# An encoder layer in split float32: one group of adaLN dots, one DMA queue and one weight-splitting step are moved

## The chip, the cores and the metric

The kernel runs on one core of one Trainium2 chip. The metric is the device time of one execution in microseconds (us); lower is better. Five engines with their own instruction streams share the work: TensorE (PE, matrix products), VectorE (DVE), ScalarE (ACT), GpSimd (POOL) and SyncE (SP, which here only starts DMA transfers). Each engine runs its stream in order, and a DMA that an engine starts waits in that stream until the buffer it writes is free.

## The reference

One layer over 1024 positions of width 1024. All arrays are float32.

```python
mod = silu(c) @ w_ada + b_ada                     # adaLN: 6 vectors of 1024
sh1, sc1, gt1, sh2, sc2, gt2 = split(mod, 6)
h = rmsnorm(x, norm1_g) * (1 + sc1) + sh1
u, v, q, k, va, gate_a, gate_b = split(h @ w_in)
a_out = gmlp_branch(u, v, ...) @ w_a              # mixing in chunks of 128 positions
b_out = window_attention_branch(q, k, va, ...) @ w_b
merged = sigmoid(gate_a) * a_out + sigmoid(gate_b) * b_out
x = x + gt1 * (merged @ w_o)
h2 = rmsnorm(x, norm2_g) * (1 + sc2) + sh2
f_gate, f_up = split(h2 @ w_ffn_in)               # 2 x 2816 columns
x = x + gt2 * ((silu(f_gate) * f_up) @ w_ffn_out)
```

## The kernel before

**Products.** Every float32 operand of a product is split into a high part, rounded to the matrix engine's float32r, and a low part, the rest. A product is then three matmuls: high by high, high by low, low by high (`mm3`). The split of a weight tile of 128 x 1024 is a "unit": SP loads it into a tile `raw`, ACT casts it into `wh`, DVE (now and then POOL) subtracts into `wl`. The three tags have three buffers each, so a unit's cast waits until the products of the unit three before it are done, and its load until that one's subtraction is done. The gates and the feed-forward use a Strassen scheme: seven block products for eight, with sums of blocks made on DVE before and after.

**Stages, in the order of time (us from the span's start).** Both halves of the sequence (512 positions each) go through projections, attention and gMLP in `half(0)` and `half(1)` (to about 394). Each ends with the *branch projections*: a loop over eight output tiles `d`, with two products of twelve matmuls a tile and one unit of `w_ab` a tile. Next come the *gates* for `d` = 2 to 7 (to about 522), by `gate_step(d, i)` for seven block products and `gate_evict(d, i)` behind each. In a gate tile DVE also splits the next tile's weights (`gate_prep_a/b/c`, `gate_sums`) and takes dot products for adaLN: `ada_half` multiplies two half rows of `w_ada` (tiles `hs`, 128 x 512) by silu(c) and sums them into one column of `mod`. A column's next rows are loaded when its `hs` buffers are free, that is, after the dots before. In tiles 3 to 5 a third `ada_half` stands between the two parts, `low_b` and `low_s`, that `gate_prep_b` leaves for the end of the tile.

Then the *output projections* (about 515 to 617): eight tiles for half 0, eight for half 1, with 24 matmuls each and one unit of `w_o` a tile. A tile's end on DVE is `x1 = gate * product + x`; the rows of x come into a tile `xs` with two buffers (L1360, `load`, SP's queue). ACT squares x1 and DVE adds the squares into `ss`; four matmuls by `ones` (`col_rstd`) turn the `ss` of half 0 into the norm, ahead of half 1's second tile. POOL's queue carries the merged rows (`hs<-md`), the stores of x1 (`x1d`) and, in three pieces of 1 MB, more rows of `w_ada`.

The *feed-forward's first product* (about 617 to 1052, over 22 tiles `f`) ends hidden tiles (`hid`) that POOL's queue stores (`tA`, `tB`), while DVE also forms sums of the output weights (`wo`, stored to `wS`). From f = 6 on, `gain_dots` works off the last eight columns of adaLN, those of gt2: rows loaded by SP into two `t` tiles, multiplied by silu(c) on POOL (`G.tensor_tensor`), summed by an ACT copy with an accumulator, finished by two small DVE instructions. The *second product* (about 1052 to the end) has 77 steps `n` of twelve matmuls; `split_step(n + 4)` splits what step n + 4 needs, `fetch(n + 12)` loads for step n + 12.

**What sets the order.** In both feed-forward products the order is written out by hand (`manual_schedule`). Elsewhere a scheduler orders each engine's stream, except where `in_order[0]` is set: there an engine keeps the order of the program. `load` (SP) always keeps that order; `store` (POOL) leaves it to the scheduler.

Of the kernel before, what the change touches and what calls it, by code (L numbers as in the profile page):

```python
# [8 lines left out]
F32 = mybir.dt.float32  # L9
# [3 lines left out]
ALU = mybir.AluOpType  # L13
# [25 lines left out]
def kernel(  # L39
# [96 lines left out]
    def load(dst, src):  # L136
        tc.keep_in_program_order(nc.sync.dma_start(dst, src))
# [13 lines left out]
    def raw_unit(src):  # L151
        r = wpool.tile([P, UNIT], F32, tag="raw", name=nm("raw"))
        load(r, src)
        return r
# [401 lines left out]
    def x_rows(hf, k):  # L556
        return xT[k * P : (k + 1) * P, hf * HALF : (hf + 1) * HALF]
# [4 lines left out]
    def added(dst, src):  # L562
        V.tensor_tensor(dst, dst, src, op=ALU.add)
# [103 lines left out]
    def gate_prep_b(d):  # L667
        w, low = begin_split(raws[d][1])
        h, l, s1 = tmp(F32R), tmp(F32R), raws[d][2]
        A.copy(h, s1)  # L670
        gunits[d] += [w, None, (h, l)]

        def rest():
            r = raws[d][0]
            added(r[:, :Q], s1)
            added(r[:, Q:], r[:, :Q])
            V.tensor_tensor(l, s1, h.bitcast(F32), op=ALU.subtract)

        return low, rest

# [51 lines left out]
    def half(hf):  # L732
# [425 lines left out]

        for d in range(KT):
            in_order[0] = d < 2 or hf == 1 and d > 5  # L1160
            if 0 < d < KT - 1:
                wab.append(unit(None, V, abr.pop(0)))
                if d + 2 + hf < KT:
                    abr.append(raw_unit(w_ab[d + 2 + hf]))
            elif d:
                if hf == 0:
                    early.append(unit(None, V, early_raw[0]))
                else:
                    for low in gate_prep_b(2):
                        low()  # L1170
            if hf and d == 5:
                gate_load(2)
            if hf and d == 6:
                gate_prep_a(2)
                gate_sums(2)
            ms = []
            for br, t in ((1, (oH, oL)), (0, (gH, gL))):
                if hf and d == KT - 1 and br == 0:
                    held.append((wab[d], t))
                    continue  # L1180
                pb = mm_bank()
                for k in range(4):
                    kc = slice(br * Q + k * P, br * Q + (k + 1) * P)
                    mm3(pb, (wab[d][0][:, kc], wab[d][1][:, kc]), (t[0][:, k, :], t[1][:, k, :]),
                        k == 0, k == 3)
                if d < 2:
                    sg = gates.pop(0)
                    V.scalar_tensor_tensor(out=sg, in0=sg, scalar=1.0, in1=pb, op0=ALU.add,
                                           op1=ALU.mult)
                    ms.append(sg)  # L1190
                else:
                    c = tmp()
                    A.copy(c, pb)
                    j = 2 * hf + br
                    nc.scalar.dma_start(pd[d][:, j * Q : (j + 1) * Q], c)
            if d < 2:
                V.tensor_tensor(ms[0], ms[0], ms[1], op=ALU.add)
                store(md[hf][d], ms[0])
            in_order[0] = hf == 1 and (d < 1 or d > 5)
            while jobs and jobs[0][0] <= d:  # L1200
                jobs.pop(0)[1]()
            in_order[0] = False
            if hf == 0:
                ada_next(d < 1)
                if d > 5:
                    early_raw.append(raw_unit((w_q[0], w_kv[0])[d - 6]))
# [33 lines left out]
    for d in range(2, KT):  # L1240
        last = d == KT - 1
        in_order[0] = True
        if d == 2:
            gate_step(d, 0)
            gate_evict(d, 0)
            held_projection()
            block_sums(3, 1, kinds)
            gate_step(d, 1)
            low_c = gate_prep_c(d)
            gate_evict(d, 1)  # L1250
            low_c()
            gate_load(d + 1)
            gate_step(d, 2)
            gate_evict(d, 2)
            branch_load(d)
            branch_load(d + 1)
            gate_step(d, 3)
            gate_evict(d, 3)
            gate_prep_a(d + 1)
            gate_step(d, 4)  # L1260
            gate_evict(d, 4)
            gate_sums(d + 1)
            low_b, low_s = gate_prep_b(d + 1)
            gate_step(d, 5)
            gate_evict(d, 5)
            low_b()
            low_s()
            continue
        gate_step(d, 0)
        gate_evict(d, 0)  # L1270
        gate_step(d - 1, 6)
        low_c = gate_prep_c(d)
        gate_evict(d - 1, 6)
        low_c()
        ada_half("hs" if not last else None)
        if not last:
            gate_load(d + 1)
        gate_step(d, 1)
        gate_evict(d, 1)
        gate_step(d, 2)  # L1280
        gate_evict(d, 2)
        if d > 2:
            if last:
                m0.extend(m_tiles(midt))
                for k in range(2):
                    m_load(m0, 0, k)
                m_src[6] = tmp()
                gating(d - 1, None, m_src[6])
            else:
                gating(d - 1)  # L1290
        if not last:
            branch_load(d + 1)
            ada_half("hs")
        gate_step(d, 3)
        gate_evict(d, 3)
        if not last:
            gate_prep_a(d + 1)
        else:
            wo_next = unit(w_o[0], V)
            for k in (0, 1):  # L1300
                m_split(m0, k)
                m_load(m0, 0, k + 2)
        gate_step(d, 4)
        gate_evict(d, 4)
        if not last:
            gate_sums(d + 1)
            low_b, low_s = gate_prep_b(d + 1)
        else:
            m_split(m0, 6)
            for k in (2, 3):  # L1310
                m_split(m0, k)
                m_load(m0, 0, k + 2)
            m_src[7] = tmp()
            gating(d, 0, m_src[7])
        gate_step(d, 5)
        gate_evict(d, 5)
        if not last:
            low_b()
            if d in (3, 4, 5):
                ada_half("hs")  # L1320
            low_s()
    in_order[0] = False
    for k in (4, 5, 7):
        m_split(m0, k)
# [5 lines left out]
    for hf in range(2):  # L1330
# [14 lines left out]
        for d in range(KT):  # L1345
# [11 lines left out]
            if hf == 1 and d in (2, 4):  # L1357
                early.append(first_unit(d // 2 - 1))
            xk = stream("xs")
            load(xk, x_rows(hf, d))  # L1360
            pw = mm_bank()
            for k in range(KT):
                if hf == 1 and (d, k) == (1, 0):
# [340 lines left out]
                            for x in "hl"]  # L1704
            split2(raws[n], *ready[n])

    again, dots = [], []

    def gain_dots(f, i):
        if f == EARLY and i == 0:  # L1710
            again.extend(stream("hs") for _ in range(2))
            for j in range(2):
                dma(again[j], silu_d[:, j * 512 : (j + 1) * 512])
        if f >= EARLY and ada_queue and i == 6:
            again[2:] = [tmp(), tmp()]
            for j in range(2):
                dma(again[2 + j], w_ada2[ada_queue[0][0] - GT1][:, j * 512 : (j + 1) * 512])
        if dots and i % 2:
            dots.pop(0)()
        if f > EARLY and ada_queue and i in (2, 4):  # L1720
            j = i // 2 - 1
            col = ada_queue[0][0]
            part = sm(16, "part")[:, :1]
            row = again[2 + j]
            G.tensor_tensor(row, row, again[j], op=ALU.mult)
            dots.append(lambda: A.activation(row, row, AF.Copy,
                                             accum_out=part if j else acc_mod[:, col : col + 1]))
            if j:
                dots.append(lambda: (added(acc_mod[:, col : col + 1], part), ada_end(col)))
                ada_queue.pop(0)  # L1730

    with tc.manual_schedule():
        U[4, 0], U[5, 0], U[0, 0], U[1, 0] = early
# [45 lines left out]
        for f, i in steps:  # L1779
# [13 lines left out]
                evict(f, i)  # L1793
            if (f, i) == (0, 5):
                evict(0, 6)
            gain_dots(f, i)
            if i == 6 or (f, i) == (0, 5):
                hidden_sums(f)
            elif f > 2:
# [1 line left out]
            if f >= EARLY:  # L1801
                e, p = divmod(7 * (f - EARLY) + i, 10)
                if e < NP and p == 0:
                    load_out(e)
                if e < NP and p == 5:
                    later.extend(lambda e=e, p=p: out_sums(e, p) for p in range(4))
            if f == NF - 1 and i > 4:
                split_step(i - 5)

# [59 lines left out]
                put(1, hf, d)  # L1869

        ngt = sm(4, "ngt")
        V.tensor_scalar(ngt, mod[:, GT2 + 4 : GT2 + 8], -1.0, None, op0=ALU.mult)

        def step_mm(n, d):
            i, e = work[n]
# [8 lines left out]
        for n, (i, e) in enumerate(work):  # L1884
# [10 lines left out]
                        step_mm(m, d)  # L1895
            split_step(n + 4)
            fetch(n + 12)
            if n in (8, 24, 40, 52):
                m = (8, 24, 40, 52).index(n)
                load_acc(m // 2, m % 2)  # L1900
# [74 lines left out]
```

## Time and profile before

| | |
|---|---|
| median of 3 runs | 1264.94 us (1264.44 to 1266.01) |
| profiled execution | 1269.63 us, span 1267.9 us |
| PE busy | 1228.1 us, 97% of the span |
| DVE busy | 919.5 us, 73% |
| ACT busy | 586.0 us, 46% |
| POOL busy | 198.9 us, 16% |
| mean granted PE clock | 0.994 |
| DMA | 236.28 MB, 186 GB/s over the span |

In a row of the timeline the first number is the start, the second the length, and the bracket at the end the idle time of that engine just before it with what ended it. In nearly all rows the line of the source is 76, that of a helper through which instructions are issued, so rows are told apart by their tiles: `wl<-raw,wh` is the low part of a unit, `mm` and `at` are PSUM banks. A matmul row of 0.39 us overlaps the next one: what counts for the rate is the distance of their starts.

### The profile page before, as it was taken

The page shows a single profiled execution, that of the slowest core. Times are in us where ns is not written, and L with a number is a line of the kernel's source. Part 1 is how long each engine was busy: PE and PEld are TensorE (multiplying, and loading weights), DVE is VectorE, ACT ScalarE, POOL GpSimd, SP SyncE. Part 2 cuts the span into 40 slices and gives each one's busy share as a digit, 9 for nine tenths or more (in the row PEclk, how much of TensorE's full clock was granted, in tenths as well). Part 3 has the DMA queues.
Part 4 walks back from the last instruction along what each step waited for, and adds up shares of the span by engine and source line. Part 5 has one row for each costly group of instructions (what it writes and reads, how often), then busy time and mean ns, then how long its engine had stood idle before and what let it go on. Part 6 is the DMA issues. An engine that isn't in the chain of part 4 may idle for free.

```text
span 1267.9 us, 15678 instructions
## 1 busy us (share of the span) xinstructions
PE 1228.1 (97%) x5634; PEld 1013.0 (80%) x5634; DVE 919.5 (73%) x1516; ACT 586.0 (46%) x970; POOL 198.9 (16%) x234
## 2 busy tenths in 40 slices
PE   5999999999999999999999998999999999999998
PEld 4888888888877877777788887778888888888887
DVE  8998884588887889775797756777766676455646
ACT  5468863367866323433454333433432334433341
POOL 1233430113441010211100011121210000010001
PEclk9999999999999999998999999999999999999999
DMA  9632168321266466765612454556644549885542
GB/s 365 261 100 77 57 213 300 120 82 51 75 197 226 133 232 213 275 215 201 258 34 100 170 195 166 183 204 222 238 164 172 195 166 337 290 322 196 188 162 100
DMA packets 78687, 236.28 MB, mean 186 GB/s; under 512 B 9361, under 2 KB 9361, under 8 KB 72594
## 3 DMA queue, kind: packets, MB, share of 16 engines
q1 hardware_dynamic: 57602, 146.67, 33.4%
q0 software_dynamic: 17552, 82.32, 18.0%
q10 hardware_dynamic: 3456, 6.29, 1.3%
q8 instruction: 44, 0.72, 0.2%
q14 instruction: 33, 0.27, 0.1%
HBM read 177.58 MB, written 57.67 MB: 186 GB/s over the span
## 4 chain that ended last, share of the span: by engine, by line
PE 72%; DVE 12%; DMA 8%; issue 4%; ACT 4%; SPq 0%; POOL 0%; ACTq 0%; DVEq 0%; POOLq 0%
PE at L76 37%; PE mm L76 35%; DVE mid L76 3%; DVE wl L76 3%; DMA raw<-in_w_o_dram 2%; ACT wh L76 2%; DMA raw<-in_w_ga_dram 1%; DMA mid<-in_w_ada_dram 1%; DVE ws L76 1%; DMA hs<-md 1%; DMA hs<-x1d 1%; DVE hid L76 1%; DMA wS<-wo 1%; DVE xs L76 1%; ACT lb L76 1%
## 5 line engine op out<-in xcount | busy, mean ns | idle before, releaser
L76 ACT CAST wh<-raw 128x1024 fp32r<-128x1024 f32 x155 | 162.2, 1050 | 175.5 <-PE mm L76 46.4
L76 DVE TENSOR_TENSOR wl<-raw,wh 128x1024 fp32r<-128x1024 f32 x141 | 172.0, 1222 | 90.5 <-ACT wh L76 87.3
L76 PE MATMUL mm<-mid,wh 128*128 128x512 f32 x696 | 215.6, 391 | 4.5 <-ACT xs L76 3.6
L76 PEld LDWEIGHTS mm<-mid,wh 128*128 128x128 f32 x696 | 130.2, 188 | 33.9 <-ACT xs L76 4.9
L76 PE MATMUL at<-j,wh 128*128 128x512 f32 x464 | 143.1, 390 | 0.1
L76 PE MATMUL mm<-mid,wl 128*128 128x512 f32 x348 | 135.7, 391 | 0.8 <-POOL wl L76 0.5
L76 PE MATMUL mm<-wh,h 128*128 128x512 f32 x384 | 129.2, 398 | 3.0 <-ACT h L76 3.0
L76 PEld LDWEIGHTS at<-j,wh 128*128 128x128 f32 x464 | 87.0, 188 | 18.6 <-ACT wh L76 0.5
L76 DVE TENSOR_TENSOR wl<-ws,wh 128x1024 fp32r<-128x1024 f32 (+1 forms) x55 | 66.0, 1200 | 44.3 <-ACT wh L76 44.3
L76 PE MATMUL mm<-j,wh 128*128 128x512 f32 x288 | 91.1, 398 | 0.3 <-ACT wh L76 0.3
L76 PE MATMUL at<-j,wl 128*128 128x512 f32 x232 | 90.4, 390 | 0.5 <-DVE wl L76 0.5
L76 PE MATMUL at<-h,wh 128*128 128x512 f32 x288 | 90.4, 396 | 0.0
L76 PEld LDWEIGHTS mm<-wh,h 128*128 128x128 f32 x384 | 71.5, 189 | 17.7 <-ACT h L76 3.9
L76 PE MATMUL mm<-h,wh 128*128 128x512 f32 x272 | 84.6, 392 | 0.0
L76 ACT CAST wh<-ws 128x1024 fp32r<-128x1024 f32 (+1 forms) x55 | 53.5, 973 | 63.0 <-DVE ws L76 49.9
L76 PEld LDWEIGHTS mm<-mid,wl 128*128 128x128 f32 x348 | 65.3, 188 | 16.0 <-DVE wl L76 1.6
L76 PE MATMUL mm<-wl,h 128*128 128x512 f32 x192 | 75.9, 395 | 0.0
L76 PEld LDWEIGHTS mm<-j,wh 128*128 128x128 f32 x288 | 55.2, 193 | 12.2 <-ACT wh L76 0.7
L76 PEld LDWEIGHTS at<-h,wh 128*128 128x128 f32 x288 | 54.5, 190 | 11.9 <-DVE mid L76 0.7
L76 DVE TENSOR_TENSOR ol<-raw,oh 128x1024 fp32r<-128x1024 f32 x30 | 36.7, 1224 | 32.7 <-ACT oh L76 32.7
L76 PEld LDWEIGHTS mm<-h,wh 128*128 128x128 f32 x272 | 50.6, 188 | 10.3
L76 PE MATMUL mm<-j,wl 128*128 128x512 f32 x144 | 57.3, 398 | 1.1 <-DVE wl L76 1.1
(279 smaller groups left out, 2564.2 us busy)
## 6 DMA issues: line engine op xcount, KB each, us to landing
raw<-in_w_gate_dram SPq DMA_DIRECT2D x28, 512.0 KB, 3.9
tA<-hid POOLq DMA_DIRECT2D x11, 1024.0 KB, 5.2
tB<-hid POOLq DMA_DIRECT2D x11, 1024.0 KB, 5.6
wo<-in_w_out_dram POOLq DMA_DIRECT2D x22, 512.0 KB, 6.2
wS<-wo POOLq DMA_DIRECT2D x11, 1024.0 KB, 5.2
raw<-wS SPq DMA_DIRECT2D x44, 256.0 KB, 3.0
raw<-tB SPq DMA_DIRECT2D x44, 256.0 KB, 3.3
raw<-in_w_out_dram SPq DMA_DIRECT2D x33, 256.0 KB, 5.1
```

The source lines that it names most:

```text
L76: ins = f(*args, **kw)
```

## The change

Four edits. (1) In `half(1)` the unit for branch tile d + 2, not d + 1, is split in tile d, and its load is started one tile earlier; `half(0)` stays. (2) In `gate_prep_b` the subtraction into `l` goes ahead of the two sums, and in tiles 3 to 5 `low_s` goes ahead of the third `ada_half`. (3) The rows of x for the output projections are loaded through POOL's queue instead of SP's. (4) The dots of gt2 leave the first product. In the second, `row_load` fetches a column's two half rows at fixed steps, and two DVE instructions that multiply and accumulate, one in each of two steps, replace the POOL multiply and the ACT sum.

```diff
@@ gate_prep_b
         def rest():
             r = raws[d][0]
+            V.tensor_tensor(l, s1, h.bitcast(F32), op=ALU.subtract)
             added(r[:, :Q], s1)
             added(r[:, Q:], r[:, :Q])
-            V.tensor_tensor(l, s1, h.bitcast(F32), op=ALU.subtract)
@@ half: branch projections
-            if 0 < d < KT - 1:
+            if 1 - hf <= d < KT - 1 - hf:
                 wab.append(unit(None, V, abr.pop(0)))
-                if d + 2 + hf < KT:
-                    abr.append(raw_unit(w_ab[d + 2 + hf]))
-            elif d:
+                if d + 2 + 2 * hf < KT:
+                    abr.append(raw_unit(w_ab[d + 2 + 2 * hf]))
+            if d == KT - 1:
@@ gates, end of a tile
             low_b()
+            low_s()
             if d in (3, 4, 5):
                 ada_half("hs")
-            low_s()
@@ output projections
-            load(xk, x_rows(hf, d))
+            store(xk, x_rows(hf, d))
@@ feed-forward, first product
-    def gain_dots(f, i):
...
-            G.tensor_tensor(row, row, again[j], op=ALU.mult)
-            dots.append(lambda: A.activation(row, row, AF.Copy,
-                                             accum_out=part if j else acc_mod[:, col : col + 1]))
...
+    AT = ((-1, 2), (7, 12), (9, 15), (14, 18), (24, 30), (30, 36), (36, 42), (42, 48))
+    def row_load(g):
+        rows2[g] = [stream("xs") if g % 2 else tmp() for _ in range(2)]
+        for j in range(2):
+            dma(rows2[g][j], w_ada2[GT2 + g - GT1][:, j * 512 : (j + 1) * 512])
...
+            if (f, i) == (NF - 2, 6):
+                row_load(0)
@@ feed-forward, second product, after fetch(n + 12)
+        def gain_dots(n):
+            for g, (at, to) in enumerate(AT):
+                if n == at:
+                    row_load(g)
+                if n in (to, to + 1):
+                    j, col = n - to, GT2 + g
+                    part = sm(16, "part")[:, :1]
+                    row = rows2[g][j]
+                    V.scalar_tensor_tensor(out=row, in0=row, scalar=1.0, in1=again[j],
+                                           op0=ALU.mult, op1=ALU.mult,
+                                           accum_out=part if j else acc_mod[:, col : col + 1])
+                    if j:
+                        added(acc_mod[:, col : col + 1], part)
+                        ada_end(col)
```

SP's queue at the start of the output projections, before: `raw` is a weight tile of `w_o`, `xs` holds rows of x.

```order
L137 DMA raw_4999<-in_w_o_dram 128x1024
L137 DMA raw_5078<-in_w_o_dram 128x1024
L137 DMA xs_5084<-in_xT_dram 128x512
L137 DMA raw_5123<-in_w_o_dram 128x1024
L137 DMA xs_5129<-in_xT_dram 128x512
L137 DMA raw_5168<-in_w_o_dram 128x1024
```

The same place of the same queue now:

```order
L137 DMA raw_4999<-in_w_o_dram 128x1024
L137 DMA raw_5078<-in_w_o_dram 128x1024
L137 DMA raw_5123<-in_w_o_dram 128x1024
L137 DMA raw_5168<-in_w_o_dram 128x1024
L137 DMA raw_5215<-in_w_o_dram 128x1024
L137 DMA raw_5260<-in_w_o_dram 128x1024
```

Between two weight tiles no load of x stands any more.

DVE where half 0's output projections end, before: `t_1066` is x1 of half 0's last tile, `ss_5077` its sum of squares, `raw_5489` and `raw_5535` are units of `w_o` for half 1, `raw_5541` is a tile of the feed-forward's gate weight, and `ms_5503<-at_5498` reads what `col_rstd` left.

```order
L76 SCALAR_TENSOR_TENSOR t_1066_5430<-mm_5405,mod,xs_5403 128x512
L76 TENSOR_TENSOR wl_5492<-raw_5489,wh_5491 128x1024
L76 TENSOR_TENSOR ss_5077<-ss_5077,t_1067_5432 128x512
L76 SCALAR_TENSOR_TENSOR mid_5446<-mm_5461,mod,xs_5459 128x512
L76 TENSOR_SCALAR ms_5503<-at_5498 128x4
L76 TENSOR_TENSOR wl_5538<-raw_5535,wh_5537 128x1024
L76 TENSOR_TENSOR j_5451<-raw_5541,j_5450 128x1024
```

And now:

```order
L76 SCALAR_TENSOR_TENSOR t_1066_5430<-mm_5405,mod,xs_5403 128x512
L76 TENSOR_TENSOR wl_5492<-raw_5489,wh_5491 128x1024
L76 TENSOR_TENSOR j_5451<-raw_5541,j_5450 128x1024
L76 TENSOR_TENSOR ss_5077<-ss_5077,t_1067_5432 128x512
L76 SCALAR_TENSOR_TENSOR mid_5446<-mm_5461,mod,xs_5459 128x512
L76 TENSOR_SCALAR ms_5503<-at_5498 128x4
L76 TENSOR_TENSOR wl_5538<-raw_5535,wh_5537 128x1024
```

The split of the gate weight now stands ahead of the last sum of squares; on ACT its cast likewise stands ahead of the last square.

POOL in the feed-forward's first product, before: `t<-t,hs` is the multiply of `gain_dots`, the rest starts transfers.

```order
L1412 DMA wS<-wo_6715 128x2048
L1412 DMA wo_6910<-in_w_out_dram 128x1024 x2
L76 TENSOR_TENSOR t_1275_6826<-t_1275_6826,hs_6711 128x512
L1412 DMA tA<-hid_6822 128x2048
L76 TENSOR_TENSOR t_1295_6968<-t_1295_6968,hs_6710 128x512
L1412 DMA tB<-hid_6829 128x2048
L76 TENSOR_TENSOR t_1296_6969<-t_1296_6969,hs_6711 128x512
```

And now:

```order
L1412 DMA wS<-wo_6711 128x2048
L1412 DMA wo_6899<-in_w_out_dram 128x1024 x2
L1412 DMA tA<-hid_6818 128x2048
L1412 DMA tB<-hid_6821 128x2048
L1412 DMA wo_7087<-in_w_out_dram 128x1024 x2
```

POOL computes nothing in this stage any more; its transfers keep their order.

More of the change, by code (lines that the diff above doesn't have):

```diff
@@ L1705, in split_step @@
             split2(raws[n], *ready[n])
-    again, dots = [], []
-    def gain_dots(f, i):
[L1710 to L1724, printed above, removed]
-            G.tensor_tensor(row, row, again[j], op=ALU.mult)
-            dots.append(lambda: A.activation(row, row, AF.Copy,
-                                             accum_out=part if j else acc_mod[:, col : col + 1]))
-            if j:
-                dots.append(lambda: (added(acc_mod[:, col : col + 1], part), ada_end(col)))
-                ada_queue.pop(0)
+    AT = ((-1, 2), (7, 12), (9, 15), (14, 18), (24, 30), (30, 36), (36, 42), (42, 48))
+    again, rows2 = [], {}
+    def row_load(g):
+        rows2[g] = [stream("xs") if g % 2 else tmp() for _ in range(2)]
+        for j in range(2):
+            dma(rows2[g][j], w_ada2[GT2 + g - GT1][:, j * 512 : (j + 1) * 512])
     with tc.manual_schedule():
@@ L1795 @@
                 evict(0, 6)
-            gain_dots(f, i)
             if i == 6 or (f, i) == (0, 5):
@@ L1806 @@
                     later.extend(lambda e=e, p=p: out_sums(e, p) for p in range(4))
+            if (f, i) == (NF - 3, 0):
+                again.extend(stream("hs") for _ in range(2))
+                for j in range(2):
+                    dma(again[j], silu_d[:, j * 512 : (j + 1) * 512])
+            if (f, i) == (NF - 2, 6):
+                row_load(0)
             if f == NF - 1 and i > 4:
@@ L1871 @@
         ngt = sm(4, "ngt")
-        V.tensor_scalar(ngt, mod[:, GT2 + 4 : GT2 + 8], -1.0, None, op0=ALU.mult)
+        def gain_dots(n):
[12 more added lines that the diff above has]
+                        ada_end(col)
+            if n == 54:
+                V.tensor_scalar(ngt, mod[:, GT2 + 4 : GT2 + 8], -1.0, None, op0=ALU.mult)
         def step_mm(n, d):
@@ L1897 @@
             fetch(n + 12)
+            gain_dots(n)
             if n in (8, 24, 40, 52):
```

## The prediction

> **What bounds the kernel now.** I read the page's busy line first, then the table by stage, then what PE waited for, then the chain and the timeline at each wait.
>
> ```profile
> PE 1228.1 (97%) x5634; PEld 1013.0 (80%) x5634; DVE 919.5 (73%) x1516; ACT 586.0 (46%) x970; POOL 198.9 (16%) x234
> ```
> ```profile
> core 0: us, PE busy (x) PEld busy (x) DVE busy (x) ACT busy (x) POOL busy (x), PEclk, DMA share, GB/s
> 345.00:410.00 65.00, 62.95 (x292) 51.20 (x291) 52.93 (x77) 43.66 (x68) 19.83 (x20) 1.00 0.64 215
> 410.00:516.00 106.00, 101.93 (x445) 82.96 (x444) 91.32 (x159) 36.77 (x51) 9.90 (x18) 1.00 0.55 184
> 516.00:576.00 60.00, 54.90 (x234) 43.46 (x234) 42.51 (x64) 23.89 (x34) 13.13 (x23) 0.98 0.80 267
> 576.00:630.00 54.00, 52.94 (x229) 43.36 (x229) 33.48 (x44) 22.16 (x29) 6.07 (x9) 0.93 0.60 219
> 730.00:860.00 130.00, 123.52 (x540) 100.65 (x539) 92.08 (x121) 46.39 (x77) 22.91 (x28) 1.00 0.53 191
> 860.00:1052.00 192.00, 192.00 (x847) 158.48 (x845) 131.78 (x185) 69.50 (x105) 24.58 (x37) 1.00 0.53 188
> 1052.00:1268.00 216.00, 210.29 (x924) 173.09 (x923) 121.70 (x123) 83.61 (x84) 10.60 (x18) 1.00 0.64 229
> ```
>
> PE sets the time, and no matmul is removed. From 860 to 1052 it never pauses: 847 matmuls in 192.00 us, 0.227 us each. Elsewhere it can only win back pauses. They are span less busy: 2.05 us in the branch projections, 4.07 in the gates, 5.10 and 1.06 in the output projections, 6.48 in the early feed-forward. Together that is 18.8 us, and the summary of PE's waits from 345 to 1052 names what ended them; its largest rows:
>
> ```profile
> PE at L76 <- DVE ss L76: 5.3, 2, 4.2
> PE at L76 <- DVE mid L76: 4.1, 3, 1.5
> ...
> PE mm L76 <- ACT xs L76: 3.6, 3, 1.7
> ```
>
> The columns are total, times, longest. All four edits aim at these rows. Besides, the clock column falls to 0.93 behind the longest wait.
>
> **Output projections (x's rows on POOL's queue).** The chain through the longest wait:
>
> ```profile
> 564.39 0.67 DVE t L76
> ...
> 565.08 0.33 SPq L137
> ...
> 565.50 4.78 DMA raw<-in_w_o_dram
> ...
> 572.58 0.69 DVE ss L76
> ```
> ```profile
> 562.59 0.73 PE L76 MATMUL mm<-j,wh 128*128 128x512 f32 x2 [0.27 <-ACT wh L76]
> 563.85 0.50 PE L76 MATMUL mm<-j,wl 128*128 128x512 f32 x1 [0.53 <-DVE wl L76]
> 573.32 1.59 PE L76 MATMUL at<-ones,ss 128*128 128x1 f32 x8 [4.20 <-DVE ss L76]
> ```
>
> SP starts the load of x's rows only when DVE has used up the older `xs`. The next `w_o` load stands behind it on SP. ACT's cast waits 4.78 us for that load, and the last square stands behind the cast. The loop closes on itself: the late unit holds back the next x1 on DVE. With x on POOL, SP is held only by its three `raw` buffers, and the `w_o` weights come well ahead. So 0.27, 0.53 and most of 4.20 us go.
>
> What is late next: the new order puts the split of a feed-forward gate weight ahead of the last square. Call T the end of half 0's last product; a tile is 24 x 0.227 = 5.44 us. That weight's load waits for the `raw` of a unit that is cast when the tile before ends (T - 5.44) and subtracted some 2.3 us later.
>
> ```profile
> L76 ACT CAST wh<-raw 128x1024 fp32r<-128x1024 f32 x155 | 162.2, 1050 | 175.5 <-PE mm L76 46.4
> L76 DVE TENSOR_TENSOR wl<-raw,wh 128x1024 fp32r<-128x1024 f32 x141 | 172.0, 1222 | 90.5 <-ACT wh L76 87.3
> ```
> ```profile
> raw<-in_w_gate_dram SPq DMA_DIRECT2D x1, 512.0 KB, 5.7
> ```
>
> With 5.7 us to land it is there at T + 2.7; cast (1.05), subtraction (1.22) and sum (0.69) give T + 5.7, and PE asks at T + 5.44. I leave 0.8 us of wait (0 to 2). The gain is 5.0 - 0.8 = 4.2 us.
>
> The clock comes on top:
>
> ```profile
> 574.77 1.20 PE L76 MATMUL mm<-j,wh 128*128 128x512 f32 x2
> ...
> 580.03 0.85 PE L76 MATMUL mm<-j,wh 128*128 128x512 f32 x2
> ```
> ```profile
> 623.25 1.02 PE L76 MATMUL at<-ones,ss 128*128 128x1 f32 x8 [1.06 <-DVE ss L76]
> 624.13 0.71 PE L76 MATMUL at<-h,wh 128*128 128x512 f32 x2
> ...
> 628.61 1.05 PE L76 MATMUL at<-ident,rcol 128*128 128x128 f32 x8
> ```
>
> Behind the pause of 4.20 us twelve matmuls take 580.03 - 574.77 = 5.26 us, not 2.72: 2.5 us lost. Behind the pause of 1.06 us twelve take 4.48: 1.8 us lost. So a short pause beside the one-column matmuls may cost too. I count 1.9 of the 2.5 us as won (bounds 0.7 and 2.5), since the new pause is nearer to none than to 1.06. The Trainium skill ("TensorE: Matmul & The Clock Gate", "Why this matters for your kernels") drops the clock only for idle gaps of more than about 3 us; by that rule all 2.5 us would be won, and the sum would be 0.6 us better. The row at 623.25 speaks against it: 1.06 us was enough there. This stage: 4.2 + 1.9 = 6.1 us (3.0 to 7.5).
>
> **Feed-forward, first product (dots leave POOL and ACT).**
>
> ```profile
> 806.55 3.96 DVE L76 TENSOR_TENSOR wl<-ws,wh 128x1024 fp32r<-128x1024 f32 x1 [0.51 <-ACT wh L76]
> ```
> ```profile
> 806.89 2.54 POOL L76 TENSOR_TENSOR t<-t,hs 128x512 f32<-128x512 f32 x2
> ```
> ```profile
> 842.12 0.63 ACT L76 ACTIVATE t<-t 128x512 f32<-128x512 f32 x1 [3.62 <-POOL t L76]
> ```
> ```profile
> 777.94 0.69 DVE L76 TENSOR_TENSOR hid<-hid 128x512 f32<-128x512 f32 x1 [5.47 <-DMA wS<-wo]
> ```
> A subtraction of 1.22 us takes 3.96 while POOL multiplies (2.54 us); PE's pause behind it is one of the 3.6 us on `xs`. At 842 ACT waits 3.62 us for POOL's product with a weight cast queued behind. Both go. The largest pause, 2.3 us, has another root: DVE waits 5.47 us for the store of `wS`, which moves beside the dots' rows; of that I leave 1.0 us. Gain: 6.48 - 1.0 = 5.4 us (3.0 to 6.5). From 860 on, with dots still running, there are no pauses, so nothing is won there.
>
> **Branch projections (units two tiles ahead).**
>
> ```profile
> 363.20 1.20 PE L76 MATMUL mm<-mid,wh 128*128 128x512 f32 x4 [0.61 <-ACT wh L76]
> 364.66 0.50 PE L76 MATMUL mm<-mid,wl 128*128 128x512 f32 x1 [0.27 <-DVE wl L76]
> 406.21 0.50 PE L76 MATMUL at<-j,wl 128*128 128x512 f32 x1 [0.53 <-DVE wl L76]
> ```
> ```profile
> 357.18 0.69 DVE L76 SCALAR_TENSOR_TENSOR t<-t,mm 128x512 f32<-128x512 f32 x1 [1.21 <-PE mm L76]
> ```
>
> The first late unit is now split a tile earlier, where DVE idles 1.21 us anyway; its 1.22 us is hidden there. If that cover fails, tile 0's evictions come 1.2 us later, still ahead of tile 2. This wins 0.88 us. Of the 0.53 at 406 I count 0.3: the earlier `l` frees the `t` tile that ACT's copy ahead of that unit's cast waits for. Gain 1.2 us (0.3 to 1.4).
>
> **Gates (`low_s` first).**
>
> ```profile
> 437.35 0.69 DVE L76 SCALAR_TENSOR_TENSOR hs<-hs,silu_c 128x512 f32<-128x512 f32 x1 [1.47 <-DMA hs<-in_w_ada_dram]
> ```
> ```profile
> 451.01 3.01 PE L76 MATMUL at<-j,t 128*128 128x512 f32 x12 [1.44 <-DVE mid L76]
> ...
> 471.52 3.02 PE L76 MATMUL at<-j,t 128*128 128x512 f32 x12 [1.17 <-DVE mid L76]
> ...
> 492.80 3.01 PE L76 MATMUL at<-j,t 128*128 128x512 f32 x12 [1.45 <-DVE mid L76]
> ```
>
> PE waits three times for an eviction on DVE, behind a backlog. Swapping two pieces of the same backlog wins only where DVE idled: in tile 3, whose dots waited 1.47 us for their rows while `low_s` could have run. That takes away the 1.44; 1.17 and 1.45 stay. The dots now start 1.9 us later, so the next dots' rows come later too; against that I set 0.2 us. Gain 1.2 us (0 to 4.1).
>
> **Second product (dots on DVE).** Sixteen multiplies of 0.69 us (the row at 437.35 is the same operation), their accumulator reads and small ends make about 1.9 us a column, 15 us in all; DVE is busy 121.70 of 216 us there, and splits run four steps (10.9 us, a step of twelve matmuls being 2.72) ahead. I put 0.3 us on the path (0 to 3); without that cover it would be up to 15. The rows' loads are 0.5 MB a column, eight times, among 229 GB/s.
>
> **Sum.** 6.1 + 5.4 + 1.2 + 1.2 - 0.3 = 13.6 us. The profiled execution is 1269.63 us (span 1267.9), so 1256.0 by it; the runs' median is 1264.94, which gives **1251.3 us**.
>
> **Rivals.** (a) Later waits take the place: the gate weight lands late, the clock still falls, `wS` holds DVE as before. With the low ends of the two large terms (3.0 and 3.0) the gain is 8.1 or less, about half of mine on balance: 1258. For it speaks that DVE stays busy 86% of the gate stage; against it, that PE's pauses end after 860. Chance 0.20.
>
> (b) Slower: POOL's queue brings x late. `xs` has two buffers, so rows are started after the x1 two tiles before and have 10.9 - 0.75 - 1.1 = 9 us until needed. If they land later, x1 waits on DVE, with the next unit's subtraction queued behind it, and PE stops in every tile. Rows of that size on POOL's queue took 4.0 us:
>
> ```profile
> hs<-md POOLq DMA_DIRECT2D x14, 256.0 KB, 4.0
> ```
>
> For a loss of over 0.2% the sixteen tiles must lose 13.6 + 2.5 = 16.1 us, 1 us each: landing in 10 us. Then it gives 1268. Chance 0.07.
>
> (c) The dots don't hide in the second product: 8 x 1.9 = 15 us on the path eats the gain, 1266. Against it speak DVE's idle 94 us. Chance 0.04.
>
> **Numbers.** My forecast has 0.69. Its own bounds and most of (a) make the range, 1246.5 to 1260. Faster by over 0.2% (2.5 us, about what a measurement of this kernel can tell): 0.69 + (a) less a little, 0.87. Within: (c) and the tail of (a), 0.05. Slower: (b) and some of (c), 0.08.
>
> **What would show it.** Right: the row `at<-ones,ss` near 570 waits under 1 us; from 730 to 860 PE is busy over 128 of 130 us; two of the three `at<-j,t` waits remain. Wrong: `xs<-in_xT` on POOL landing in over 9 us, DVE waiting for it, or PE pausing before 1100.

## The result, and the profile after

The changed kernel takes 1253.25 us (median of 5 runs, 1249.84 to 1257.47) against 1264.94 us for the kernel before. The ratio is 0.9908, with a 95% interval of 0.9883 to 0.9933: 11.6 us less, where 13.6 were forecast. Its profiled execution took 1254.18 us (span 1252.4 us), near its median; the one of before had been 4.7 us over its own, so the two profiles differ by 15.5 us, more than the kernels do.

The busy line of the changed kernel's page and its table by stage (the last stretch begins 16 us earlier now, as that stage does):

```profile
PE 1222.5 (98%) x5634; PEld 1011.4 (81%) x5634; DVE 915.0 (73%) x1548; ACT 578.7 (46%) x938; POOL 184.6 (15%) x234
```
```profile
345.00:410.00 65.00, 63.23 (x294) 51.40 (x293) 52.52 (x77) 43.89 (x69) 19.97 (x20) 1.00 0.67 212
410.00:516.00 106.00, 104.30 (x457) 85.11 (x456) 93.54 (x162) 38.38 (x53) 12.05 (x22) 1.00 0.61 204
516.00:576.00 60.00, 56.70 (x239) 46.35 (x238) 41.34 (x62) 24.30 (x33) 17.99 (x31) 0.94 0.81 273
730.00:860.00 130.00, 129.44 (x570) 106.53 (x570) 84.97 (x119) 44.91 (x62) 11.73 (x22) 1.00 0.54 194
1036.00:1252.00 216.00, 210.74 (x927) 173.26 (x925) 134.52 (x171) 84.12 (x85) 10.62 (x18) 1.00 0.68 247
```

The early feed-forward has become whole: 0.56 us without work where 6.48 were. The gates went from 4.07 to 1.70. The output projections still miss 3.30. Their clock column reads 0.94 where 0.98 stood, but only because the slow matmuls, behind 576 us before, now fall inside the stretch: over 516 to 630 us it is 0.96 before and 0.97 now. The second product is busy 210.74 us with 927 matmuls, as before (210.29 with 924). The summary of what PE waited for from 345 to 1037 names the rest:

```profile
PE at L76 <- DVE ss L76: 3.3, 1, 3.3
PE mm L76 <- ACT mid L76: 0.8, 1, 0.8
PE at L76 <- DVE mid L76: 0.6, 1, 0.6
```

One wait stands out, and it is the one that was to go. The chain through it:

```profile
556.31 0.06 DVE t L76
...
556.98 1.23 DVE wl L76
...
558.22 6.74 DMA raw<-in_w_gate_dram
...
564.98 1.05 ACT j L76
...
566.06 0.56 DVE j L76
566.62 0.58 issue
567.20 0.69 DVE ss L76
...
567.94 1.50 PE at L76 x8
```

The loop through x's rows is gone from it. The load of the feed-forward gate weight has taken its place: it starts when the subtraction at 556.98 has freed its `raw`, and takes 6.74 us; its cast and subtraction stand ahead of the last sum.

### The profile page after: what moved, and what is told of

The parts are those of the page before. It is cut to its first block, busy times and chain, and to the rows that moved or that the text cites. A ratio compares the mean times of both kernels' runs of the same rounds, so it can differ in the third digit from the quotient of the medians.

```text
span 1252.4 us, 15649 instructions
## 1 busy us (share of the span) xinstructions
PE 1222.5 (98%) x5634; PEld 1011.4 (81%) x5634; DVE 915.0 (73%) x1548; ACT 578.7 (46%) x938; POOL 184.6 (15%) x234
## 4 chain that ended last, share of the span: by engine, by line
PE 63%; DVE 11%; DMA 11%; issue 9%; ACT 5%; POOL 1%; SPq 0%; ACTq 0%; DVEq 0%; POOLq 0%
PE at L76 34%; PE mm L76 29%; DVE mid L76 3%; DVE wl L76 3%; ACT wh L76 2%; DMA raw<-in_w_out_dram 1%; DMA raw<-in_w_ga_dram 1%; DMA hs<-in_w_ada_dram 1%; DVE hs L76 1%; DMA mid<-in_w_ada_dram 1%; DMA xs<-in_w_ada_dram 1%; DVE t L76 1%; ACT lb L76 1%; DVE raw L76 1%; DMA hs<-in_xT_dram 1%
## 5 line engine op out<-in xcount | busy, mean ns | idle before, releaser
L76 DVE TENSOR_TENSOR wl<-ws,wh 128x1024 fp32r<-128x1024 f32 (+1 forms) x55 | 62.0, 1127 | 44.0 <-ACT wh L76 44.0
L76 ACT ACTIVATE xs<-xs 128x512 f32<-128x512 f32 x21 | 13.3, 633 | 96.9 <-DVE xs L76 96.9
```

Of the source, the lines that this page charges most:

```text
L76: ins = f(*args, **kw)
```

## The experiments

Stage by stage, worked out from PE's rows: the us between the same two matmuls of its stream, less those in the first profile of before (negative: shorter). The stages begin at the matmuls that stood there at 345, 410, 516, 640 and 1052 us; each column is one profiled execution. The last matmul of the gates here is the one ahead of the stop near 513 us, so that stop counts with the output projections:

```
                   before  changed  low_   x_on_  dots_  dots_first  branch_two  gate_   branch_  both_   x_two
                   again            first  pool   moved  _on_dve     _ahead      later   undone   mended  _on_sp
branch projections   0.03   -0.29  -0.47   0.04  -0.01    -0.01       -0.04       0.05   -0.42   -0.41   -0.46
gates                1.70   -4.25  -4.24  -1.35  -1.70    -3.91       -2.58      -3.30   -4.06   -4.43   -3.46
output projections  -4.36   -4.56  -3.28  -6.95  -3.30    -4.99       -2.65     -11.11   -3.39  -10.20  -12.31
first product       -0.71   -7.13  -0.13   0.02  -7.18    -1.41       -0.48      -7.00   -6.99   -6.96   -7.81
second product       0.04    0.00  -0.03  -0.02   0.08    -0.03        0.02       0.08    0.12    0.12    0.08
```

The first column is the kernel before against itself: the gates and the output projections move by 2 and 4 us from one execution to the next, the feed-forward by under 1. A profile alone therefore decides only in the feed-forward; elsewhere the runs' ratios have to.

**The kernel before again (before_again).** 

> The kernel before, unchanged, profiled once more. It tells which of the pauses in its first profile belong to the kernel and which to that one execution (1269.63 us, 4.7 us over the median). Theory (the first profile was an unlucky one): the slow matmuls behind half 1's ones-matmuls (1.8 us) are absent, as they are in three kernels that left the output projections' queues alone, and the three waits of the gate stage are smaller by 1 to 2 us in all; the five pauses of the feed-forward's first product and the pause of about 4.2 us in the output projections stay. Rival (all of it is the kernel's): every pause comes back within 0.3 us.

A second set of runs gave a ratio of 1.0013 (1.0001 to 1.0025) to the first, so 0.13% is nothing here. PE's rows in the output projections and in the gates:

```profile
574.78 1.87 PE L76 MATMUL at<-ones,ss 128*128 128x1 f32 x8 [4.18 <-DVE ss L76]
576.51 1.20 PE L76 MATMUL mm<-j,wh 128*128 128x512 f32 x2
...
580.87 0.63 PE L76 MATMUL mm<-j,wh 128*128 128x512 f32 x2
...
623.23 1.02 PE L76 MATMUL at<-ones,ss 128*128 128x1 f32 x8 [0.44 <-DVE ss L76]
```
```profile
452.42 3.01 PE L76 MATMUL at<-j,t 128*128 128x512 f32 x12 [1.63 <-DVE mid L76]
472.92 3.01 PE L76 MATMUL at<-j,t 128*128 128x512 f32 x12 [1.17 <-DVE mid L76]
494.11 4.61 PE L76 MATMUL at<-j,t 128*128 128x512 f32 x12 [1.85 <-DVE mid L76]
```

The wait of 4.2 us belongs to the kernel. The one of half 1 is 0.44 instead of 1.06 us, and no slow matmuls follow it: the 1.8 us lost there in the first profile were that execution's. On the gates the expectation was wrong: all three waits are there, 4.65 us together against 4.06, and the twelve matmuls behind the last take 4.61 us where the others take 3.01: the clock fell there (last section).

**The four edits one by one**, each alone in the kernel before.

x's rows on POOL's queue (x_on_pool):

```diff
-            load(xk, x_rows(hf, d))
+            store(xk, x_rows(hf, d))
```

> The kernel before with only x's rows on GpSimd's queue. Theory (each edit acts in its own stage): PE's two short waits before half 0's last product go (0.27 and 0.53 us), the long one before the ones-matmuls shrinks only from 4.2 to about 3.3 us, because the split of the feed-forward gate weight now stands ahead of the last square; the 1.06 us wait of half 1 and the slow matmuls behind it (1.8 us) go, because the weights of w_o come ahead there too. Gain 4.5 us in the output projections, nothing elsewhere. Rival (the output projections gained because the gate stage ended earlier): the 1.06 us wait stays, gain under 2 us.

Ratio 0.9965 (0.9951 to 0.9979), 4.4 us. From 520 to 640 us PE waits 2.60 us ahead of the ones-matmuls and nowhere else:

```profile
570.25 1.05 PE L76 MATMUL at<-ones,ss 128*128 128x1 f32 x8 [2.60 <-DVE ss L76]
571.17 0.71 PE L76 MATMUL mm<-j,wh 128*128 128x512 f32 x2
...
575.52 0.70 PE L76 MATMUL mm<-j,wh 128*128 128x512 f32 x2
```

The gain is as the theory had it, but its profile shows why no single row proves the size: half 1's wait is absent here, and in the kernel before it was 1.06 us in one profile and 0.44 in the other.

The dots alone (dots_moved), with the AT steps, `row_load` and `gain_dots` as in the diff of the change:

> The kernel before with only the gt2 dots moved to the second product. Theory: all five pauses of PE in the first product (6.5 us by the busy table, 7.3 by the matmuls' starts) go down to under 1.3 us together, the one behind the store of wS too, since the small transfers and POOL's multiplies were what made them; nothing is added in the second product. Gain 6 to 7 us. Rival (the wS pause is fixed by the time at which the stage starts, which the other edits shift): it stays at 2.3 us, gain 4 us. Rival (sixteen multiplies on DVE cost in the second product): PE pauses of 0.69 us appear between steps 2 and 49.

Ratio 0.9955 (0.9942 to 0.9969), 5.7 us. The five pauses of the first product come to 0.2 us in all, the one behind `wS` being gone too, and the second product does not change (0.08 us). The first theory holds, 0.3 us under its lower end.

`low_s` and the subtraction first (low_first), the two hunks on the gates:

> The kernel before with only the subtraction and low_s ahead of the sums and the dots. Theory (the swap wins wherever the evictions waited for the dots' backlog): all three waits before at<-j,t (1.44, 1.17, 1.45 us) fall to 0.6 us in all, gain 3.5 us, and about 1 us is given back at the end of the stage by a new wait on ACT. Rival (the recorded forecast): only the first of the three goes, gain 1.2 us.

Ratio 0.9974 (0.9963 to 0.9986), 3.3 us. One wait is left of three:

```profile
472.60 3.02 PE L76 MATMUL at<-j,t 128*128 128x512 f32 x12 [0.57 <-DVE mid L76]
```

In this profile nearly all is gone, against the forecast's one of three. The profile alone doesn't carry that: dots_first_on_dve (below) leaves the gates as they were, and its gates are 3.91 us shorter too, with waits of 0.56 and 0.34 us. Over all twelve profiles PE's waits ahead of `at<-j,t` add up to 0.90 to 4.65 us in the six without the swap (mean 2.98) and to 0 to 1.53 us in the six with it (mean 0.72). The ratio's interval, 1.8 to 4.7 us, leaves out the forecast 1.2. The wait on ACT at the end of the stage did not come with this edit.

The branch units two tiles ahead (branch_two_ahead), the first hunk of `half`:

> The kernel before with only half 1's branch units split two tiles ahead. Theory (one late unit is exchanged for another): the waits of 0.61 and 0.27 us in tile 2 go, and waits of 0.2 and 0.53 us appear at the last unit of the stage, where DVE works off the gates' first sums; net within 0.4 us of nothing. Rival (the recorded forecast): gain 1.2 us, no new wait.

Ratio 1.0017 (1.0002 to 1.0031), no more than the kernel before shows against itself. The 0.61 and 0.27 us in tile 2 are gone, and the changed kernel's PE rows show what came:

```profile
398.86 0.73 PE L76 MATMUL mm<-j,wh 128*128 128x512 f32 x2 [0.17 <-ACT wh L76]
400.12 0.50 PE L76 MATMUL mm<-j,wl 128*128 128x512 f32 x1 [0.53 <-DVE wl L76]
...
406.65 0.50 PE L76 MATMUL at<-j,wl 128*128 128x512 f32 x1 [0.53 <-DVE wl L76]
```

0.88 us saved, 0.70 added, and the 0.53 at 406 not touched. The four ratios add up to 0.9911, the whole change measured 0.9908: no sign that the edits get in each other's way.

**Mending what was left.** The gate weight's two pieces one tile later in the changed kernel (gate_later):

```diff
-            if hf == 1 and d in (2, 4):
+            if hf == 1 and d in (3, 5):
                 early.append(first_unit(d // 2 - 1))
```

> The changed kernel with the two pieces of the feed-forward gate weight split one tile later, which puts the first behind the last square and sum of half 0. Theory (PE waits 3.3 us only because the load of that weight ends late and stands ahead of the last sum): the sum is ready before half 0's last product ends, the wait falls under 0.3 us, and the slow matmuls behind it (2.5 us) go with it; gain 5.5 us. Rival (the one-column matmuls slow the clock with or without a wait): the 2.5 us stay, gain 3.3 us. Rival (the last x1 itself is late): a wait over 2 us stays, gain about 1 us.

1249.19 us, 0.9878 (0.9864 to 0.9891) of the kernel before: 4.1 us under the changed kernel. PE's rows:

```profile
566.34 0.95 PE L76 MATMUL at<-ones,ss 128*128 128x1 f32 x8
567.15 0.70 PE L76 MATMUL mm<-j,wh 128*128 128x512 f32 x2
...
570.00 0.62 PE L76 MATMUL mm<-j,wh 128*128 128x512 f32 x2
```

No wait; the next twelve matmuls take 570.00 - 567.15 = 2.85 us. In the changed kernel twelve took 574.56 - 569.29 = 5.27:

```profile
567.94 1.50 PE L76 MATMUL at<-ones,ss 128*128 128x1 f32 x8 [3.30 <-DVE ss L76]
569.29 1.20 PE L76 MATMUL mm<-j,wh 128*128 128x512 f32 x2
...
574.56 0.92 PE L76 MATMUL mm<-j,wh 128*128 128x512 f32 x2
```

So the load in front of the sum was the cause, and the slow matmuls go with the wait; the one-column matmuls by themselves cost nothing. The stage gains 6.6 us between the two profiles, by the runs' medians 4.1 (3.8 by the two ratios): some executions of the changed kernel must lose less there than the profiled one. The fastest, 1249.84 us, had a mean granted clock of 1.000, the profiled one 0.997. Without the wait the four runs lie within 1.1 us of each other, those of the changed kernel within 7.6.

The branch hunk undone in the changed kernel (branch_undone):

> The changed kernel with the branch units as before. Theory (the edit exchanges one late unit for another): the waits of 0.61 and 0.27 us come back, those at the last unit of the stage go (0.2 and 0.53); the time stays within 1.5 us, and may be up to 2 us lower, as the edit alone measured 0.17% slower. Rival (the recorded forecast): 1.2 us slower.

1252.77 us, 0.9911 (0.9896 to 0.9926): the edit is worth nothing that can be measured. The waits of 0.61 and 0.25 us in tile 2 are back, and those of 0.17 and 0.53 near 399 are gone, as the theory had it.

Both together (both_mended):

> The changed kernel with the gate weight split one tile later and the branch units as before. Theory: the gains of the two add up, 5 to 7 us less than the changed kernel. Rival (the clock stays slow and the branch edit is worth its forecast): 2 us less.

1248.12 us, 0.9870 (0.9856 to 0.9883): 5.1 us under the changed kernel (4.8 by the ratios, at the lower edge of the expectation), and the best ratio of all. Against gate_later alone it is 1.1 us, inside both intervals.

**What made the early feed-forward pause.** The kernel before with its dots left in the first product, but on DVE (dots_first_on_dve):

```diff
-            G.tensor_tensor(row, row, again[j], op=ALU.mult)
-            dots.append(lambda: A.activation(row, row, AF.Copy,
-                                             accum_out=part if j else acc_mod[:, col : col + 1]))
+            V.scalar_tensor_tensor(out=row, in0=row, scalar=1.0, in1=again[j],
+                                   op0=ALU.mult, op1=ALU.mult,
+                                   accum_out=part if j else acc_mod[:, col : col + 1])
```

> The kernel before, its gt2 dots left in the first product with their rows loaded where they were, but the multiply taken from GpSimd and the sum from ScalarE: one VectorE instruction does both. It splits what moving the dots brought into the multiplies and the row loads. Theory (two causes): the pauses near 790, 812, 846 and 852 us, which came from GpSimd's multiplies, go (4.5 us by the matmuls' starts), while the pause behind the store of wS, which lands in 7.7 to 8.2 us beside the rows against 6.4 to 6.7 without them, stays at 1.2 to 2.4 us; gain 3 to 5 us. Rival (the multiplies are the one cause): the wS pause goes too, gain 5.7 us as with the dots moved. Rival (any dots at all between the evictions are too much for VectorE there): the pauses stay, no gain.

Ratio 0.9974 (0.9956 to 0.9993), 3.3 us. From 730 to 870 PE waits once, and its timeline shows the price:

```profile
772.55 0.79 PE L76 MATMUL mm<-h,wl 128*128 128x512 f32 x1 [2.97 <-DVE wl L76]
773.14 1.05 PE L76 MATMUL mm<-h,wh 128*128 128x512 f32 x2
...
778.26 0.84 PE L76 MATMUL at<-h,wh 128*128 128x512 f32 x2
```

The pauses near 790, 812, 846 and 852 us are gone: they came from the multiplies on POOL and the sums on ACT that waited for them, which this edit moves together. The one behind `wS` is not: DVE still waits for that store. The store of `wS` by the DMA view from 755 to 790, in the kernel before, in the changed one and here:

```profile
wS<-wo POOLq DMA_DIRECT2D x1, 1024.0 KB, 8.2
```
```profile
wS<-wo POOLq DMA_DIRECT2D x1, 1024.0 KB, 6.7
```
```profile
wS<-wo POOLq DMA_DIRECT2D x1, 1024.0 KB, 9.5
```

The other profiles agree. In the six kernels that load the dots' rows there, that store took 7.6 to 9.5 us to land and PE paused 1.07 to 2.97 us; in the six that don't, it took at most 6.7 us and PE paused at most 0.15 us. So the rows beside the store are the second cause, as far as these runs go; rows without any dots were not tried. The change moved rows and multiplies in one edit.

**The new stop at the end of the gates.** In the changed kernel ACT waits for the merged rows, and PE for ACT (rows of ACT, of PE, then of POOL's queue):

```profile
512.59 1.34 ACT L76 CAST mid<-hs 128x512 fp32r<-128x512 f32 x2 [2.11 <-DMA hs<-md]
```
```profile
513.26 0.49 PE L76 MATMUL mm<-mid,wh 128*128 128x512 f32 x1 [0.83 <-ACT mid L76]
```
```profile
508.40 1.14 POOL L140 DMA_DIRECT2D hs<-md  x2 [1.79 <-DVE mid L76]
509.53 0.73 POOL L140 DMA_DIRECT2D mid<-in_w_ada_dram  x1
```

A 1 MB load of `w_ada` starts right behind the two. In x_two_on_sp the mended kernel loads x's rows of the first two tiles by SP again:

```diff
-            store(xk, x_rows(hf, d))
+            (load if hf == 0 and d < 2 else store)(xk, x_rows(hf, d))
```

> The changed kernel with both mends (gate weight later, branch as before), and x's rows of half 0's first two tiles back on SyncE's queue. It asks what makes ScalarE wait 2 us for the merged rows near 512 us, for which PE then stops 1.4 us in all. Theory (the first loads of x on GpSimd's queue let the 1 MB load of w_ada start beside the merged rows instead of behind them, and let SyncE load w_o at the same time): with the two loads back the stop falls under 0.5 us, gain about 1 us. Rival (the traffic is there either way): the stop stays within 0.3 us of 1.4, no gain. Rival (the loads of w_o are held up again by x's buffers): waits of 0.3 to 0.5 us come back before 565 us, up to 1 us slower.

```profile
511.48 0.54 POOL L140 DMA_DIRECT2D hs<-md  x1 [0.27 <-issue]
513.84 0.73 POOL L140 DMA_DIRECT2D mid<-in_w_ada_dram  x1 [1.82 <-DMA hs<-md]
```
```profile
515.14 0.50 PE L76 MATMUL mm<-mid,wh 128*128 128x512 f32 x1 [0.21 <-DVE mid L76]
```

The big load is back behind the merged rows, and PE's stop falls to 0.21 us: the theory holds for the stop. That the stop comes with x's rows on POOL's queue is seen in x_on_pool too, where PE waits 0.70 and 0.23 us there; the kernel before, low_first, dots_moved and branch_two_ahead have no such stop. Whether the queue's order or SP's earlier `w_o` loads decide stays open, since the edit restores both. In the time it is not to be seen: 1247.86 us, ratio 0.9876 (0.9856 to 0.9897), beside 0.9870 for both_mended.

## Why the prediction was right, and which of its steps were not

The sign, the sum (13.6 against 11.6 us) and the main mechanisms held: the loop through x's rows is gone, and so are the pauses of the first product; 1253.25 lies inside 1246.5 to 1260. That the sum came so near is partly luck: by the single edits its terms miss by 0.6, -1.7, 2.1 and at least -1.2 us, and the misses largely cancel. Of the three signs of being right one came true, PE's 129.44 busy us from 730 to 860; the row near 570 waits 3.30 us instead of under 1, and of the `at<-j,t` waits one is left, not two. Term by term:

- **First and second product: 5.1 forecast (5.4 - 0.3), 5.7 measured.** Both roots were named. The residue of 1.0 us left for `wS` was too much in the changed kernel, where `wS` lands in 6.7 us, and the 0.3 us for the second product did not appear: the sixteen multiplies took 0.68 us each as priced, and splits were far enough ahead. Rival (c) is out.
- **Output projections: 6.1 forecast, 4.4 measured.** The step that failed is the wait that would be late next. The prediction named it, the gate weight's split ahead of the last square, but reckoned 0.8 us (0 to 2); it measured 3.30. Write T for the time a tile (5.44 us) before PE asks, as there: PE came free at 567.94 - 3.30 = 564.64, so T is 559.2. The load was to start at T - 3.0 and to land in 5.7; it started at 558.22, T - 1.0, and took 6.74. The subtraction that frees its `raw` stood behind the tile's x1 on DVE, which the step left out; 2.0 us for the start and 1.0 for the landing, on top of the 0.3 that the working itself gave (5.7 - 5.44, taken as 0.8), come to 3.3. The 1.9 us of clock hung on that wait and so were not won in the profiled execution. Gate_later shows both when the wait is gone.
- **Gates: 1.2 forecast, 3.3 measured.** The failed step is that the swap wins only where DVE idled for its dots, in tile 3. That DVE idled for them in tile 3 alone was so in the first profile; in the second it waited for their rows in tiles 3, 4 and 5:

```profile
438.78 0.69 DVE L76 SCALAR_TENSOR_TENSOR hs<-hs,silu_c 128x512 f32<-128x512 f32 x1 [1.87 <-DMA hs<-in_w_ada_dram]
...
459.28 0.69 DVE L76 SCALAR_TENSOR_TENSOR hs<-hs,silu_c 128x512 f32<-128x512 f32 x1 [0.99 <-DMA hs<-in_w_ada_dram]
...
480.00 0.69 DVE L76 SCALAR_TENSOR_TENSOR hs<-hs,silu_c 128x512 f32<-128x512 f32 x1 [1.24 <-DMA hs<-in_w_ada_dram]
```

  With `low_s` ahead of the dots no wait for these rows is longer than 0.53 us in any of the six profiles. In the first profile of before DVE idled in tiles 4 and 5 too, but for casts, in rows behind the first and second stop that had been put down as a backlog:

```profile
452.35 1.23 DVE L76 TENSOR_TENSOR wl<-raw,wh 128x1024 fp32r<-128x1024 f32 x1 [1.39 <-ACT wh L76]
...
473.64 1.23 DVE L76 TENSOR_TENSOR wl<-raw,wh 128x1024 fp32r<-128x1024 f32 x1 [2.17 <-ACT wh L76]
```

  A reading is that PE's stops delay themselves: an eviction late on DVE stops PE, ACT's cast waits for PE's weights, and DVE waits for the cast. In the second profile the same two rows idle 0.30 and 0.27 us although PE stops as long, so this is at most a part. That the edit by itself wins 3.3 us is shown; how it divides between rows and casts was not tried and stays open.
- **Branch: 1.2 forecast, nothing measured.** The late unit of tile 2 went as reckoned. The last unit of the stage became late in its place, which the prediction did not look for: counted from the matmul that stood at 345 us, its cast on ACT starts at 52.2 us in the changed kernel and at 52.1 in the one before, so it did not move, while PE gets there 1.5 us sooner (52.76 instead of 54.24) and finds the unit not ready. The end of the stage was held by that cast, not by the two waits alone.
- **Rivals.** (a), later waits take over, happened in the output projections above all, and in small in the branch projections. (b), x landing late on POOL's queue, did not: from 510 to 575 its rows landed in 5.2 us (median), against the 10 at which it decides. Its queue did cost something else, the stop at 513 us.

```profile
xs<-in_xT_dram POOLq DMA_DIRECT2D x10, 256.0 KB, 5.2
```

- **The baseline.** Reckoning from one profiled execution 4.7 us over its median counted pauses that the second profile does not have; in the output projections it differs from the second profile by 4.4 us.

## What to carry to other kernels

When a wait is taken away, price the next one as carefully as the first: follow the buffer that its load needs to the instruction that frees it, with all that stands ahead of that on its engine. Which waits an execution shows can change from one to the next, so an edit may take away more of them than one profile names; and a profile of before should be taken twice, to learn which stages move by themselves. An edit that moves two things (rows and multiplies, here) is best tried with each alone.

## What the runs showed of the hardware

How many matmuls run slowly does not follow the length of PE's pause. Beside the one-column matmuls, twelve matmuls took 2.85 us with no pause (gate_later), 4.35 behind 2.60 us (x_on_pool: 575.52 - 571.17) and 5.27 behind 3.30, but only 4.36 behind 4.18 us (before_again: 580.87 - 576.51). Without such matmuls, they took 5.12 behind 2.97 us (dots_first_on_dve: 778.26 - 773.14).

The granted clock shows what does decide. From 345 us to the last matmul, nine of the twelve profiles have it at 0.50 for 3.4 or 6.8 us once or twice, and the three without a pause ahead of the ones-matmuls (gate_later, both_mended, x_two_on_sp) not at all. In one profile such stretches start whole multiples of 3.41 us apart: in the first of before at 573.66 and 624.86 us, 15 times 3.41. Cut at these multiples, PE's time looks like this around the pause of 1.85 us in before_again and around that of 2.25 us in the first profile of before (after the length stand PE's busy us; the granted clock is the third number from the end):

```profile
491.04:494.45 3.41, 1.55 (x8) 0.97 (x7) 2.94 (x9) 0.64 (x1) 1.34 (x3) 1.00 0.90 299
494.45:497.86 3.41, 3.41 (x10) 2.65 (x9) 2.94 (x4) 1.04 (x2) 0.00 (x0) 0.50 0.99 350
```
```profile
775.04:778.46 3.42, 2.53 (x12) 1.76 (x10) 0.52 (x1) 0.00 (x0) 0.00 (x0) 1.00 0.97 374
778.46:781.87 3.41, 2.05 (x9) 1.71 (x10) 3.20 (x5) 1.31 (x4) 0.00 (x0) 1.00 0.10 40
```

The shorter pause fell into one stretch, which left PE busy for 1.55 of 3.41 us, and the next stretch ran at half the clock. The longer pause was shared by two stretches, busy for 2.53 and 2.05 us, and the clock stayed at 1.00 behind them too. With 1.68 us busy it stayed as well (x_on_pool, 490.33 to 493.74). Where one-column matmuls make up part of the busy time it fell after 2.00 us (x_on_pool, 568.84 to 572.25) and 2.35 us (before, 621.44 to 624.86). So in these traces the price of a pause hangs on PE's busy share in a fixed stretch of 3.41 us, and on how the pause falls across it. The Trainium skill ("TensorE: Matmul & The Clock Gate", "What's actually happening") has a free-running window of about 3.4 us. The traces agree with the window, but not with the rest: there the clock falls after an idle window, and here 1.55 us of work in it did not prevent the fall.

The spread of the runs fits in part: 7.6 us in the changed kernel and 1.1 in gate_later, but 3.6 in x_two_on_sp, which has no such pause either.

A subtraction on DVE beside POOL's multiplies had taken 3.96 us, that is 1.22 of its own and 2.54 of the multiplies and 0.2. The Trainium skill ("SBUF — State Buffer", "SBUF: two separate sides") describes the port pair that these two engines share as an exclusive lock for a whole instruction. The sum agrees; and in dots_first_on_dve, which took the multiplies off POOL, no subtraction from 730 to 860 us takes that long.
